# Mixer output projection in seven products: chains spread over steps, and the order of the first product

## The chip, the cores and the metric

The kernel runs on one core of one Trainium2 chip, as one launch. The metric is the device time of that launch in microseconds (us), the median of several runs. The profile names the core's engines PE (matrix products; PEld is its weight load), DVE, ACT and POOL (elementwise work), and SP, whose queue issues the kernel's DMAs.

## What is computed

One layer of a hybrid encoder: a sparse attention and a state-space (SSD) mixer read the same input, their outputs are projected, merged under sigmoid gates and projected once more, and a gated feed-forward block follows, all over 1024 positions of width 1024 in float32. The part around the change is this (the reference, cut):

```python
y_a = sparse_mla_attention(...) @ w_o_attn
y_b = ssd_mixer(...) @ w_o_ssd          # ssd_mixer ends in rmsnorm over 2048 columns
mix = (sigmoid(g_a) * y_a + sigmoid(g_b) * y_b) @ w_out
x = x + gate_m * rmsnorm(mix, post_norm_mix)
h2 = rmsnorm(x, pre_norm_ffn) * (1.0 + scale_f) + shift_f
u_gate, u_up = split(h2 @ w_ffn_in, 2)
f = (silu(u_gate) * u_up) @ w_ffn_out
x = x + gate_f * rmsnorm(f, post_norm_ffn)
```

## The kernel before

Activations lie transposed: 128 channels on the partitions, 512 positions (one half) in a tile. A float32 operand of a product is split in two parts, a high part rounded to the matrix engine's format (ACT writes it) and the rest (DVE or POOL subtracts); a product of four 128-row blocks is then twelve matmuls of 128x512: high by high, high by low, low by high (`P3`).

**The stage.** After the SSD mixer, `y @ w_o_ssd` is made by a seven-product scheme, with block products named 1, 5, 6, 7, 3, 4, 2, and `merged @ w_out` in two passes A and B, one per half of the positions. A list `seq` holds 88 steps `(name, m, h)`: `m` is the block of output channels, `h` the half of the four-plus-four row blocks that the step multiplies. Each step is twelve matmuls. The order is 1, 5, 6, 7, 3 (steps 0 to 39, eight each), A (40 to 55), 4 and 2 (56 to 71), B (72 to 87). Before the change product 1 runs its steps as (m=0,h=0), (m=0,h=1), (m=1,h=0) and so on.

**One pass of the loop** (`for i in range(len(seq))`, L1374 on) issues, in this order: the load of a SSD output tile for the next product (`y_act`, into pool EV), the raw weights of step i+5 (`wo_load`; four raw buffers), whatever `pre[i]` holds (loads of gates, of the attention branch, of x), the twelve matmuls of step i (`wo_mm`), the weight sum of step i+3 (`wo_sum`, DVE), the high part of the loaded tile (ACT, L1386), the split of the weights of step i+2 (`wo_split`: ACT `whi`, POOL `wlo`; three buffers each), then whatever `post[i]` holds, and last the low part of the loaded tile (DVE, L1391).

**Order.** The whole loop, and before the change also the preload in front of it (raw weights of steps 0 to 4, the eight tile pairs of product 1, the weight splits of steps 0 and 1), stands under `in_order` for PE, ACT, DVE, POOL and SP: each engine gets these instructions in exactly the order in which the code issues them. Outside of `in_order` a planner orders instructions by their place in the code and by when it reckons that they are ready; it may weave the fixed chain with the end of the SSD mixer, which is not under `in_order`.

**What `post` holds before.** Each of these is issued whole in one pass:

- `merge`: DVE multiplies by the gate (L1282), POOL or DVE adds the attention branch (L1283), ACT makes the high part `mgh`, DVE the low part `mgl` (through `split`, L243 and L244). Sixteen of them, eight before A and eight before B.
- `gate_fn`: ACT sigmoid, POOL multiplies by `rys` (L1274). `rys_make` at steps 4 and 6: the SSD norm's sums on PE (`rstd`, L257), a DVE and a POOL instruction for the reciprocal root, four PE transposes that spread it (`rspread`, L268), ACT copies it (L1307). The sums come from `ysq`, which the SSD mixer's last chunks still add to (L1071).
- `mixed`: ACT copies an output of A or B and squares it (L1299, L1300), DVE adds the squares (L1302).
- `x_first` (q0+2 to q0+12, where q0 = 56 is the first step of product 4): DVE scales (L1314), DVE or POOL adds x (L1315), ACT squares (L1316), DVE sums (L1318), SP stores. It needs `prm`, made by `rstd` at q0 and `rspread` at q0+1.
- `h_first` (b0+1 to b0+8, b0 = 72): DVE scales by `pr2` (L1323; its `rstd` and `rspread` at q0+14 and q0+15), ACT high part (L1160), DVE low part (L1161), ACT shift in place (L1163): the input of the FFN.

The gates and x wait in pool Q (26 tiles), which also holds the sixteen split tiles of products 5, 7 and 4. PSUM has three banks in one pool (`bank_d`) and five in another (`bank`); product 1's output tiles take three of the first and one of the second.

Of the kernel before, what the change touches and what calls it, by code (L numbers as in the profile page):

```python
# [65 lines left out]
def build(tc, a, dbg=None, stop=99, slots=None):  # L66
# [1090 lines left out]
    def ffn_input(b, t, h2):  # L1157
        if b == 0:
            hi, lo = H_("h2h", dt=F32R), H_("h2l", dt=F32R)
            S.activation(hi, h2, AF.Identity, bias=mod[:, 24 + t:25 + t])  # L1160
            V.scalar_tensor_tensor(lo, h2, mod[:, 24 + t:25 + t], f(hi), op0=OP.add, op1=OP.subtract)  # L1161
            X[("11", "21")[t // 4]][t % 4] = hi, lo
        S.activation(h2, h2, AF.Identity, bias=mod[:, 24 + t:25 + t])  # L1163

# [115 lines left out]
    def merge(x, t, y, eng):  # L1280
        g = gates.pop((x, t))
        V.tensor_tensor(g, y, g, op=OP.mult)  # L1282
        eng.tensor_tensor(g, g, yas.pop((x, t)), op=OP.add)  # L1283
# [29 lines left out]
    def x_first(t):  # L1313
        V.scalar_tensor_tensor(mixA[t], mixA[t], gm[:, t:t + 1], keep["prm"], op0=OP.mult, op1=OP.mult)  # L1314
        (V if t % 2 else G).tensor_tensor(x1[t], mixA[t], x1[t], op=OP.add)  # L1315
        S.activation(mixA[t], x1[t], AF.Square)  # L1316
        if t:
            V.tensor_tensor(mixA[t], mixA[t], sq_["x"], op=OP.add)  # L1318
# [9 lines left out]

    end = {n: [pos[n, m, 1] + 1 for m in range(4)] for n in PRODUCT}
    for m in range(4):  # L1330
        post[end["1"][m]].append(lambda m=m: S.activation(c11[m], U(m), AF.Copy))
        post[end["5"][m]].append(lambda m=m: S.activation(c22[m], outs["5", m], AF.Copy))
        post[end["6"][m]].append(lambda m=m: V.tensor_tensor(c12[m], U(m), c22[m], op=OP.add))
        post[end["7"][m]].append(lambda m=m: V.tensor_tensor(c22[m], U(m), c22[m], op=OP.add))
        post[end["3"][m]].append(lambda m=m: V.tensor_tensor(c12[m], outs["3", m], c12[m], op=OP.add))
        post[end["2"][m]].append(lambda m=m: V.tensor_tensor(c11[m], outs["2", m], c11[m], op=OP.add))
# [6 lines left out]
    a0, b0 = pos["A", 0, 0], pos["B", 0, 0]
    for q, m in enumerate((0, 1, 2, 3)):
        plan_merge("B", 4 + m, end["4"][m], a0 - 1 + 2 * q, a0 + 1 + 2 * q, lambda m=m: U(m), G)
        plan_merge("B", m, end["2"][m], a0 + 7 + 2 * q, a0 + 9 + 2 * q, lambda m=m: c11[m], V)
    for t in range(8):
        for n, i0 in (("A", a0), ("B", b0)):
            post[min(i0 + 2 * t + 2, len(seq) - 1)].append(lambda n=n, t=t: mixed(n, t))
    q0 = pos["4", 0, 0]  # L1350
    post[q0].append(lambda: kept_as("rm", lambda: rstd([sq_["A"]], D)))
    post[q0 + 1].append(lambda: kept_as("prm", lambda: rspread(keep["rm"])))
    for t, at in enumerate((2, 3, 5, 6, 8, 9, 11, 12)):
        pre[q0 + at - 4].append(lambda t=t: x_ask(t))
        post[q0 + at].append(lambda t=t: x_first(t))
    post[q0 + 14].append(lambda: kept_as("r2", lambda: rstd([sq_["x"]], D)))
    post[q0 + 15].append(lambda: kept_as("pr2", lambda: rspread(keep["r2"])))
# [4 lines left out]
    X = {n: [None] * 4 for n in ("11", "21", "22", "1", "2", "3", "4")}  # L1362
    with in_order(mybir.EngineType.PE, mybir.EngineType.Activation, mybir.EngineType.DVE,
                  mybir.EngineType.Pool, mybir.EngineType.SP):
        for i in range(4):
            wo_load(i)
        for j in range(8):
            y_act("1", j)
            if j < 2:
# [4 lines left out]
        for i in range(len(seq)):  # L1374
            if i + 1 in feeds:
                y_act(*feeds[i + 1])
            wo_load(i + 5)
            for fn in pre[i]:
                fn()
            wo_mm(i)  # L1380
            wo_sum(i + 3)
            if i in feeds:
                n, j = feeds[i]
                hi, lo = ((H_, Q)[PRODUCT[n] % 2]("a" + k, None, F32R) for k in "hl")
                r = als.pop((n, j))
                S.activation(hi, r, AF.Copy)  # L1386
            wo_split(i + 2)
            for fn in post[i]:
                fn()
            if i in feeds:  # L1390
                V.tensor_tensor(lo, r, f(hi), op=OP.subtract)  # L1391
# [122 lines left out]
    with in_order(mybir.EngineType.PE):  # L1514
# [7 lines left out]
        for t in range(8):  # L1522
            ffn_input(1, t, y1[t])
# [279 lines left out]
```

## Time and profile before

| | |
|---|---|
| median of 3 runs | 2474.64 us (2472.56 to 2478.26) |
| the profiled execution | 2472.58 us |
| its span, first to last instruction | 2470.8 us |
| TensorE clock granted, mean of the span | 0.983 |
| busy: PE, DVE, ACT, POOL | 95%, 66%, 51%, 44% |

The span is cut by the profile from the first to the last instruction of the program; 1.8 us of the execution's time lie around it. Busy shares count matmuls from issue to end, and two in a row overlap, so a stage is better judged by the number of matmuls in it. The views used below are the page, the table by stretches of time, the timeline, and the instruction groups of a stretch ("xN" is a count; behind the bar stand the busy time, the mean of one in ns, and the idle time of the engine just before these instructions, with what ended it).

### The profile page before, as it was taken

What the parts mean: (1) busy time and instruction counts of PE and PEld (TensorE: products, weight loads), DVE (VectorE), ACT (ScalarE), POOL (GpSimd) and SP (SyncE); (2) the same over time, 40 slices, a digit from 0 to 9 for tenths busy, and PEclk for the clock granted to TensorE, in tenths of its full rate; (3) what the DMA queues carried; (4) which work ended last, traced back from release to release, by engine and by line L of the source; (5) the groups of instructions that cost most, each with busy time, mean ns of one, the idle gap of its engine ahead of it and who ended that gap; (6) DMA issues with size and microseconds to landing.
All of it is one profiled execution on the core that took longest, in us unless ns stands there. A gap on an engine that the chain in (4) does not pass through costs nothing. (4 is left out here: it accounts for less than half of the span.)

```text
span 2470.8 us, 35232 instructions
## 1 busy us (share of the span) xinstructions
PE 2355.7 (95%) x11782; PEld 1898.6 (77%) x11782; DVE 1640.7 (66%) x3150; ACT 1267.5 (51%) x2440; POOL 1099.1 (44%) x869
## 2 busy tenths in 40 slices
PE   7999999999999999999999986989899999999997
PEld 5888888887888877777777765767678788888877
DVE  4467775697765566765667775864557777556786
ACT  3456665667355554555666664534456222335442
POOL 1421112222344346732445433766368555554465
PEclk9999999999999999999999998999999999999999
DMA  7123112422323223314779776646365555328665
GB/s 267 65 89 126 63 66 94 154 90 95 105 95 105 88 101 103 104 49 133 224 246 310 251 233 216 230 154 200 98 234 174 184 176 182 124 99 290 229 213 167
DMA packets 238918, 384.54 MB, mean 156 GB/s; under 512 B 23649, under 2 KB 91921, under 8 KB 238737
## 3 DMA queue, kind: packets, MB, share of 16 engines
q1 hardware_dynamic: 238016, 381.72, 46.5%
q8 instruction: 93, 1.52, 0.3%
q14 instruction: 89, 0.72, 0.1%
q10 hardware_dynamic: 720, 0.58, 0.1%
HBM read 284.13 MB, written 101.21 MB: 156 GB/s over the span
## 5 line engine op out<-in xcount | busy, mean ns | idle before, releaser
L150 POOL TENSOR_TENSOR wlo<-wraw,whi 128x512 fp32r<-128x512 f32 x146 | 200.1, 1371 | 501.6 <-ACT whi L149 459.5
L1412 PE MATMUL p<-xh,wr 128*128 128x512 f32 x880 | 274.1, 389 | 1.9 <-DVE u L1479 1.9
L1406 POOL TENSOR_TENSOR wr<-a,wr 128x512 fp32r<-128x512 f32 x110 | 156.3, 1429 | 125.1 <-ACT wr L1405 94.5
L244 POOL TENSOR_TENSOR wlo<-wraw,whi 128x512 fp32r<-128x512 f32 x97 | 139.1, 1439 | 127.1 <-ACT whi L243 111.4
L1412 PEld LDWEIGHTS p<-xh,wr 128*128 128x128 f32 x880 | 165.2, 188 | 36.7 <-DVE u L1479 2.4
L1412 PE MATMUL p<-xl,wr 128*128 128x512 f32 x440 | 171.2, 389 | 0.0
L149 ACT ACTIVATE whi<-wraw 128x512 fp32r<-128x512 f32 x146 | 91.3, 627 | 122.3 <-issue 39.5
L777 ACT ACTIVATE lg<-lg,mx 128x256 f32<-128x256 f32 (+7 forms) x128 | 98.6, 771 | 100.3 <-DVE mx L774 96.8
L1405 ACT ACTIVATE wr<-a 128x512 fp32r<-128x512 f32 x110 | 68.5, 629 | 144.5 <-PE p L1412 122.9
L1258 PE MATMUL pos<-ah,whi 128*128 128x512 f32 x224 | 94.1, 420 | 21.9 <-ACT whi L243 14.9
L1412 PE MATMUL p<-h2h,wr 128*128 128x512 f32 x352 | 113.3, 398 | 0.0
L244 POOL TENSOR_TENSOR wlo<-ws,whi 128x512 fp32r<-128x512 f32 x57 | 84.7, 1490 | 61.3 <-ACT whi L243 55.8
L637 ACT ACTIVATE junk<-acc,cand__2182 128x1024 bf16<-128x1024 f32 (+2 forms) x96 | 86.2, 898 | 45.7 <-DVE cand__2182 L680 29.9
L1583 PE MATMUL pfo<-ah,wlo 128*128 128x512 f32 x264 | 103.2, 391 | 1.9 <-POOL wlo L244 1.9
L588 DVE SCALAR_TENSOR_TENSOR acc<-rel,widx,acc 128x384 f32<-128x384 f32 (+2 forms) x90 | 87.0, 986 | 24.7 <-ACT rel L583 24.5
L1583 PE MATMUL pfo<-ah,whi 128*128 128x512 f32 x264 | 103.0, 390 | 0.4 <-ACT whi L243 0.4
L1583 PE MATMUL pfo<-al,whi 128*128 128x512 f32 x264 | 102.7, 389 | 0.0
L583 ACT ACTIVATE rel<-prel 128x512 f32<-128x512 f32 (+3 forms) x160 | 77.2, 524 | 48.1 <-PE prel L582 44.5
L315 POOL TENSOR_TENSOR adaw<-adaw,cs 128x512 f32<-128x512 f32 x64 | 66.5, 1042 | 78.0 <-DMA adaw<-ada_w 70.7
L1258 PE MATMUL pos<-ah,wlo 128*128 128x512 f32 x224 | 94.1, 420 | 6.9 <-POOL wlo L244 6.5
L1412 PEld LDWEIGHTS p<-xl,wr 128*128 128x128 f32 x440 | 82.6, 188 | 17.0
L1672 DVE TENSOR_TENSOR al<-al,ah 128x512 fp32r<-128x512 f32 x66 | 71.3, 1082 | 34.1 <-ACT ah L1667 31.8
(604 smaller groups left out, 7500.8 us busy)
## 6 DMA issues: line engine op xcount, KB each, us to landing
wraw<-w_in SPq DMA_DIRECT2D x130, 256.0 KB, 2.6
a<-w_ffn_in SPq DMA_DIRECT2D x120, 256.0 KB, 3.2
al<-d_a SPq DMA_DIRECT2D x77, 256.0 KB, 4.0
wraw<-w_ffn_out SPq DMA_DIRECT2D x66, 256.0 KB, 3.9
adaw<-ada_w SPq DMA_DIRECT2D x64, 256.0 KB, 2.7
al<-d_ac SPq DMA_DIRECT2D x32, 512.0 KB, 4.5
wraw<-w_o_ssd SPq DMA_DIRECT2D x56, 256.0 KB, 3.5
al<-d_y SPq DMA_DIRECT2D x56, 256.0 KB, 4.3
```

What stands on the lines that cost most here:

```text
L149: behind(S.activation(hi[:, :kt], raw[:, :kt], AF.Copy))
L150: behind(G.tensor_tensor(lo[:, :kt], raw[:, :kt], f(hi[:, :kt]), op=OP.subtract))
L244: (lo_eng or V).tensor_tensor(lo, src, f(hi), op=OP.subtract)
L583: S.activation(rel[:, 512 * b:512 * b + w_], pr[:, 0:w_], AF.Relu)
L588: V.scalar_tensor_tensor(acc[i][:, 0:n], rel[:, 0:n], ws, acc[i][:, 0:n], op0=OP.mult, op1=OP.add)
L637: S.activation(jk, y, AF.Sign, scale=-1.0, bias=a_, accum_out=o)
L777: S.activation(lg[:, 0:n], lg[:, 0:n], AF.Exp, scale=-1.0, bias=m, accum_out=mx[:, 3:4])
L1258: T.matmul(p, w[wi][:, q], xs[k][xi], start=n in "1532AB" and h == 0 and q == 0 and x == 0, stop=h == 1 and q == 3 and x == 2, skip_group_ ...
L1406: G.tensor_tensor(w[:, 1], src, f(w[:, 0]), op=OP.subtract)
L1412: T.matmul(p, w[:, wi, i], X[x][i][xi], start=start and i == 0 and k == 0, stop=i == 3 and k == 2, skip_group_check=True)
L1583: T.matmul(o, w[wi][:, P * m:P * m + P], x[xi][:, cl], start=j == 0 and k == 0, stop=j == NP - 1 and k == 2)
L1672: V.tensor_tensor(lo, r, f(hi), op=OP.subtract)
```

## The change

Four things change, all in this stage.

1. Product 1 runs its steps as all four `m` with h=0, then all four with h=1. So steps 0 to 3 read only the first four tile pairs of the SSD output.
2. The preload stands ahead of `in_order`. The loop runs four passes longer, for parts that come after the last step.
3. Every chain of `post` is cut in parts which are issued in successive passes. A merge: multiply at i, add at i+1, high and low part at i+2 (nearer together for the last ones before A and B). The gate's scaling by `rys` comes one pass after the sigmoid. `mixed`: the sum one pass after the squares. `x_first`: five parts in five passes, starting one or two passes later. `h_first`: scale, then high and low part, then shift, in three passes, from q0+20 on (before: b0+1 = q0+17).
4. Each normaliser is split: `rstd` at i, `rspread` at i+2; `rys` is copied at i+3. They stand at steps 5 and 9 (before: 4 and 6), at q0+1 (q0) and q0+17 (q0+14).

```diff
     FIRST, LAST = 1, 0
-    seq = [(n, m, h) for part, ms in (("15673", 4), ("A", 8), ("42", 4), ("B", 8)) for n in part for m in range(ms) for h in BS]
+    seq = [("1", m, h) for h in BS for m in range(4)]
+    seq += [(n, m, h) for part, ms in (("5673", 4), ("A", 8), ("42", 4), ("B", 8)) for n in part for m in range(ms) for h in BS]
...
+    def at(i, fn, *args):
+        post[i].append(lambda: fn(*args))
...
-    def merge(x, t, y, eng):
-        g = gates.pop((x, t))
-        V.tensor_tensor(g, y, g, op=OP.mult)
-        eng.tensor_tensor(g, g, yas.pop((x, t)), op=OP.add)
-        MG.setdefault(x, {})[t] = split(H_, g, "mg")
+    def merge(x, t, y):
+        V.tensor_tensor(gates[x, t], y(), gates[x, t], op=OP.mult)
+
+    def merge_add(x, t, eng):
+        eng.tensor_tensor(gates[x, t], gates[x, t], yas.pop((x, t)), op=OP.add)
+
+    def merge_hi(x, t):
+        hi, lo = H_("mgh", dt=F32R), H_("mgl", dt=F32R)
+        S.activation(hi, gates[x, t], AF.Copy)
+        MG.setdefault(x, {})[t] = hi, lo
+
+    def merge_lo(x, t):
+        hi, lo = MG[x][t]
+        V.tensor_tensor(lo, gates.pop((x, t)), f(hi), op=OP.subtract)
...
+        at(fn, gate_fn, x, t)
+        at(fn + 1, gate_scale, x, t)
+        pre[i - 5].append(lambda: ya_load(x, t))
+        at(i, merge, x, t, y)
+        at(i + steps[0], merge_add, x, t, eng)
+        at(i + steps[1], merge_hi, x, t)
+        at(i + steps[1], merge_lo, x, t)
...
+    def normaliser(i, name, sq, n):
+        at(i, kept_as, ("r", name), lambda: rstd([sq()], n))
+        at(i + 2, kept_as, name, lambda: rspread(keep["r", name]))
...
-    post[4].append(lambda: rys_make(FIRST))
-    post[6].append(lambda: rys_make(LAST))
+    for i, b in ((5, FIRST), (9, LAST)):
+        normaliser(i, ("pry", b), lambda b=b: ysq[b], D_INNER)
+        at(i + 3, rys_keep, b)
...
+        plan_merge("A", 4 + m, end["7"][m] + 1, G_LOAD[m], G_FN[m], lambda m=m: c22[m], G, (1, 2))
+        plan_merge("A", m, end["3"][m], G_LOAD[4 + m], G_FN[4 + m], lambda m=m: c12[m], V if m > 1 else G,
+                   ((1, 2), (1, 2), (0, 1), (0, 0))[m])
+        plan_merge("B", 4 + m, end["4"][m], a0 - 1 + 2 * m, a0 + 1 + 2 * m, lambda m=m: U(m), G, (1, 2))
+        plan_merge("B", m, end["2"][m], a0 + 7 + 2 * m, a0 + 9 + 2 * m, lambda m=m: c11[m], V,
+                   ((0, 1), (0, 1), (0, 1), (0, 0))[m])
     for t in range(8):
...
+            at(i0 + 2 * t + 2, mixed, n, t)
+            at(i0 + 2 * t + 3, mixed_sum, n, t)
+    normaliser(q0 + 1, "prm", lambda: sq_["A"], D)
+    for t, i in enumerate((4, 5, 7, 8, 9, 11, 12, 13)):
+        pre[q0 + i - 4].append(lambda t=t: x_ask(t))
+        for n, fn in enumerate((x_scale, x_add, x_square, x_sum, x_store)):
+            at(q0 + i + n, fn, t)
+    normaliser(q0 + 17, "pr2", lambda: sq_["x"], D)
     for t in range(8):
-        post[b0 + 1 + t].append(lambda t=t: h_first(t))
+        at(q0 + 20 + t, h_scale, t)
+        at(q0 + 21 + t, ffn_hi, t)
+        at(q0 + 21 + t, ffn_lo, t)
+        at(q0 + 22 + t, ffn_shift, t)
...
+    for i in range(4):
+        wo_load(i)
+    for j in range(8):
+        y_act("1", j)
+        acts["1"][j] = split(H_, als.pop(("1", j)), "a")
+        if j < 2:
+            wo_split(j)
+    y_act(*feeds[0])
+    wo_load(4)
     with in_order(mybir.EngineType.PE, mybir.EngineType.Activation, mybir.EngineType.DVE,
                   mybir.EngineType.Pool, mybir.EngineType.SP):
...
-        for i in range(len(seq)):
+        for i in range(len(post)):
...
-            wo_mm(i)
+            if i < len(seq):
+                wo_mm(i)
```

More of the change, by code (lines that the diff above doesn't have):

```diff
@@ L1155, in residual_steps, with ffn_hi, ffn_lo, ffn_shift @@
         yield
[L1157 to L1162, printed above, removed]
+    X = {n: [None] * 4 for n in ("11", "21", "22", "1", "2", "3", "4")}
+    def ffn_hi(t):
+        hi, lo = H_("h2h", dt=F32R), H_("h2l", dt=F32R)
+        S.activation(hi, x1[t], AF.Identity, bias=mod[:, 24 + t:25 + t])
+        X[("11", "21")[t // 4]][t % 4] = hi, lo
+    def ffn_lo(t):
+        hi, lo = X[("11", "21")[t // 4]][t % 4]
+        V.scalar_tensor_tensor(lo, x1[t], mod[:, 24 + t:25 + t], f(hi), op0=OP.add, op1=OP.subtract)
+    def ffn_shift(t, x=None):
+        h2 = (x or x1)[t]
         S.activation(h2, h2, AF.Identity, bias=mod[:, 24 + t:25 + t])
@@ L1271, in gate_fn, with gate_scale @@
     def gate_fn(x, t):
-        g = gates[x, t]
-        S.activation(g, g, AF.Sigmoid)
-        G.tensor_tensor(g, g, rys[FIRST if x == "A" else LAST], op=OP.mult)
+        S.activation(gates[x, t], gates[x, t], AF.Sigmoid)
+    def gate_scale(x, t):
+        G.tensor_tensor(gates[x, t], gates[x, t], rys[FIRST if x == "A" else LAST], op=OP.mult)
     def ya_load(x, t):
@@ L1303, in mixed, with rys_keep @@
         sq_[n] = sq
-    def rys_make(b):
+    def rys_keep(b):
         rys[b] = wp.tile([P, 4, P], F32, name="rys", tag=("uraw", "uh")[b], bufs=1).rearrange("p k m -> p (k m)")
-        S.activation(rys[b], rbank(ysq[b], D_INNER), AF.Copy)
+        S.activation(rys[b], keep["pry", b], AF.Copy)
     def x_ask(t):
@@ L1343, in build @@
[L1343 to L1346, printed above, removed]
+        at(end["1"][m], lambda m: S.activation(c11[m], U(m), AF.Copy), m)
+        at(end["5"][m], lambda m: S.activation(c22[m], outs["5", m], AF.Copy), m)
+        at(end["6"][m], lambda m: V.tensor_tensor(c12[m], U(m), c22[m], op=OP.add), m)
@@ new lines, in build @@
+        at(end["7"][m], lambda m: V.tensor_tensor(c22[m], U(m), c22[m], op=OP.add), m)
+        at(end["3"][m], lambda m: V.tensor_tensor(c12[m], outs["3", m], c12[m], op=OP.add), m)
+        at(end["2"][m], lambda m: V.tensor_tensor(c11[m], outs["2", m], c11[m], op=OP.add), m)
+    for i, b in ((5, FIRST), (9, LAST)):
+        normaliser(i, ("pry", b), lambda b=b: ysq[b], D_INNER)
+        at(i + 3, rys_keep, b)
+    G_LOAD, G_FN = (4, 5, 6, 7, 15, 16, 17, 18), (10, 11, 13, 14, 18, 19, 21, 22)
@@ new lines, in build @@
+    a0, b0, q0 = pos["A", 0, 0], pos["B", 0, 0], pos["4", 0, 0]
+    for m in range(4):
+        plan_merge("A", 4 + m, end["7"][m] + 1, G_LOAD[m], G_FN[m], lambda m=m: c22[m], G, (1, 2))
[4 more added lines that the diff above has]
+                   ((0, 1), (0, 1), (0, 1), (0, 0))[m])
@@ L1347, in build @@
     for t in range(8):
         for n, i0 in (("A", a0), ("B", b0)):
[L1349 to L1355, printed above, removed]
@@ L1522, in build @@
         for t in range(8):
[L1523 removed]
+            ffn_shift(t, y1)
         ffn_sums(x1, y1)
```

45 lines of the change are left out of this document (13 added, 32 removed).

## The prediction

> **What bounds the kernel now.** The page first: PE is the busiest engine by far. I then cut the stage of the change with the table by stretches of time, counting only its matmuls (L1258; a count may take in one that overlaps an edge).
>
> ```profile
> PE 2355.7 (95%) x11782; PEld 1898.6 (77%) x11782; DVE 1640.7 (66%) x3150; ACT 1267.5 (51%) x2440; POOL 1099.1 (44%) x869
> ```
>
> ```profile
> core 0: us, PE busy (x) PEld busy (x), PEclk, DMA share, GB/s
> 1450.20:1514.90 64.70, 7.16 (x24) 4.25 (x23) 0.87 0.53 170
> 1514.90:1549.20 34.30, 27.67 (x96) 21.32 (x97) 0.84 0.84 285
> 1549.20:1595.50 46.30, 46.30 (x206) 38.24 (x205) 1.00 0.65 212
> 1595.50:1652.20 56.70, 48.00 (x181) 34.84 (x180) 0.94 0.46 155
> 1690.30:1706.00 15.70, 14.23 (x62) 11.17 (x62) 1.00 0.39 123
> 1706.00:1758.50 52.50, 40.55 (x145) 28.97 (x144) 0.90 0.48 160
> 1772.10:1808.40 36.30, 29.81 (x121) 21.71 (x119) 1.00 0.30 99
> ```
>
> In the third stretch nothing stalls: 17 steps of twelve matmuls take 46.3 us, so a step costs 46.3/17 = 2.72 us, a matmul 0.227. By that price the others are too long. Steps 2 to 9: 34.3 where 8 x 2.72 = 21.8, excess 12.5. Steps 27 to 41: 56.7 against 40.8, excess 15.9. Steps 56 to 60: 15.7 against 13.6, excess 2.1. Steps 61 to 72: 52.5 against 32.6, excess 19.9. Steps 78 to 87: 36.3 against 27.2, excess 9.1. Together 59.5 us; what lies between ran at 2.72. Before that, from 1450.2 to 1514.9, only steps 0 and 1 ran. What follows the stage runs PE without a gap, so a stage that ends earlier ends the kernel earlier:
>
> ```profile
> 1860.00:1900.00 40.00, 40.00 (x178) 33.14 (x177) 33.62 (x29) 22.84 (x43) 36.00 (x24) 1.00 0.47 159
> ```
>
> **The start (order of product 1, preload, rys).** The timeline of the stage's beginning:
>
> ```profile
> 1448.61 2.19 ACT L243 ACTIVATE ah<-al 128x512 fp32r<-128x512 f32 x4
> ...
> 1463.70 0.51 PE L1258 MATMUL pos<-ah,whi 128*128 128x512 f32 x1 [4.40 <-ACT ah L243]
> ...
> 1483.79 0.66 PE L1025 MATMUL pyd<-al,X 128*64 128x256 f32 x4 [4.11 <-DVE al L986]
> 1493.86 0.66 PE L1025 MATMUL pyd<-al,X 128*64 128x256 f32 x4 [3.38 <-DVE al L986]
> 1502.91 0.50 PE L1258 MATMUL pos<-ah,whi 128*128 128x512 f32 x1 [2.57 <-ACT ah L243]
> ...
> 1506.56 0.40 PE L1258 MATMUL pos<-ah,wlo 128*128 128x512 f32 x1
> ...
> 1512.41 0.63 ACT L1049 ACTIVATE ysqt<-zy 128x512 f32<-128x512 f32 x1 [4.43 <-POOL zy L1046]
> ...
> 1513.82 0.42 DVE L1071 TENSOR_TENSOR ysq<-ysq,ysqt 128x256 f32<-128x256 f32 x1
> ...
> 1514.27 0.61 ACT L243 ACTIVATE whi<-wraw 128x512 fp32r<-128x512 f32 x1
> ...
> 1514.93 0.80 PE L1258 MATMUL pos<-ah,whi 128*128 128x512 f32 x1 [7.98 <-ACT whi L243]
> ...
> 1523.42 0.63 ACT L1386 ACTIVATE ah<-al 128x512 fp32r<-128x512 f32 x1 [5.98 <-DMA al<-d_y]
> ...
> 1525.43 0.95 PE L257 MATMUL p<-ones,ysq 128*128 128x1 f32 x8
> ...
> 1528.73 0.65 PE L268 MATMUL prn<-ident,r 128*128 128x128 f32 x4 [2.35 <-POOL r L262]
> ...
> 1529.59 0.63 PE L1258 MATMUL pos<-al,whi 128*128 128x512 f32 x1
> 1530.01 0.63 PE L1258 MATMUL pos<-ah,wlo 128*128 128x512 f32 x1
> ...
> 1532.57 0.45 PE L1258 MATMUL pos<-ah,wlo 128*128 128x512 f32 x1
> ```
>
> PE finishes step 1 at 1506.6, when the last SSD tile of product 1 is there, then stands 8 us for the weights of step 2: ACT has their split in its fixed order behind the SSD mixer's last squares (1512.41), which wait for POOL. Later it stands 2.35 us in the middle of `rys`, and comes back slow: two matmuls start 0.42 us apart, not 0.227, until about 1532.6.
>
> After: steps 0 to 3 need only tiles 0 to 3, split by about 1451 (1448.61 and on), so their 48 matmuls and the weight splits behind them go into the idle gaps of the SSD chunks. Step 4 waits for the eighth tile as step 1 did and ends at 1506.6, step 5 at 1509.3. Then comes a new wait: `rstd` of `rys` now stands behind step 5 on PE, and needs `ysq`, last added to at 1513.82 + 0.42 = 1514.2; steps 6 on queue behind it. It ends at 1515.2. Steps 6 to 9 cost 10.9, one set of transposes 0.65, the second `rstd` 0.95, and a slow restart like that of 1529 to 1532.6, some 8 matmuls x 0.2 = 1.6 us: step 10 begins at 1529.3. The eighth tile of product 5, converted by 1523.42 + 0.63, is needed only at the end of step 9 and does not bind. To this I add 2 us because 24 more matmuls (5.4 us) and five weight splits share the SSD mixer's last chunks, whose period is 10.1 us (1483.79 to 1493.86) with 3.4 to 4.1 us of PE idle in each: the bounds are 0 and the 5.4 us. So 1531.3 against 1549.2, **18 us** gained; bounds 21.5 (no delay, no slow restart) and 0 (the planner leaves the order as it is).
>
> **The merges into A (steps 27 to 41).** Instruction groups of that stretch, ACT, DVE and POOL:
>
> ```profile
> L243 ACT ACTIVATE mgh<-sgb 128x512 fp32r<-128x512 f32 x8 | 5.1, 631 | 29.0 <-POOL sgb L1283 26.3 <-DVE sgb L1283 2.7
> ```
>
> ```profile
> L244 DVE TENSOR_TENSOR mgl<-sgb,mgh 128x512 fp32r<-128x512 f32 x8 | 5.5, 692 | 17.6 <-ACT mgh L243 17.6
> L1335 DVE TENSOR_TENSOR acc<-pos,acc 128x512 f32<-128x512 f32 x4 | 2.7, 682 | 0.0
> ```
>
> ```profile
> L1283 POOL TENSOR_TENSOR sgb<-sgb,yal 128x512 f32<-128x512 f32 x7 | 9.0, 1288 | 4.3 <-DVE sgb L1282 4.3
> ```
>
> Eight merges cost ACT 29.0 us of standing and DVE 17.6, and the next `whi` and weight sums wait behind them. With a pass between the parts these waits go. What is late next is the throughput of DVE and POOL together. Where both are full the timeline shows:
>
> ```profile
> 1557.56 1.78 DVE L1190 TENSOR_TENSOR ws<-ws,wraw 128x512 f32<-128x512 f32 x1
> 1559.27 1.78 DVE L1391 TENSOR_TENSOR al<-al,ah 128x512 fp32r<-128x512 f32 x1
> ```
>
> ```profile
> 1557.05 3.44 POOL L244 TENSOR_TENSOR wlo<-ws,whi 128x512 fp32r<-128x512 f32 x2
> ```
>
> A DVE instruction on two SBUF tiles takes 0.69 us when POOL is still and 1.78 beside it; in alternation a pair goes every 1.70 us. Counting the changed code, passes 27 to 41 issue 21 POOL instructions (15 `wlo`, 6 adds), 35 such DVE ones (7 low parts of tiles, 10 weight sums, 8 multiplies, 8 low parts of merges, 2 adds) and 8 that read PSUM. So 21 pairs x 1.70 = 35.7, plus 14 x 0.69 = 9.7, makes 45.4 us if the PSUM readers lie beside POOL, 50.8 if none does (8 x 0.68, as L1335). PE wants 40.8, and weights are split two steps ahead, a lead of 5.4 less 1.9 for `whi` and `wlo` (0.61 + 1.29): 3.5. So 1.1 to 6.5 us of stall remain; I take 4, nearer the middle since both engines mix the two. The steps between 10 and 26 keep their contents and their 2.72.
>
> **Residual and merges into B (steps 56 to 72).** The same view of 1706.0 to 1758.5, then the timeline:
>
> ```profile
> L243 ACT ACTIVATE mgh<-sgb 128x512 fp32r<-128x512 f32 x6 | 3.8, 632 | 18.0 <-POOL sgb L1283 9.4 <-DVE sgb L1283 8.6
> L1316 ACT ACTIVATE acc<-xr 128x512 f32<-128x512 f32 x6 | 3.8, 631 | 14.5 <-POOL xr L1315 8.2 <-DVE xr L1315 6.3
> ```
>
> ```profile
> 1702.02 0.33 SPq L1311 DMA_DIRECT2D xr<-xT  x1
> ...
> 1709.75 0.33 SPq L1311 DMA_DIRECT2D xr<-xT  x1
> ...
> 1716.44 0.50 PE L1258 MATMUL pos<-ah,whi 128*128 128x512 f32 x1 [1.62 <-ACT whi L243]
> ...
> 1749.29 1.05 PE L257 MATMUL p<-ones,acc 128*128 128x1 f32 x8 [2.87 <-DVE acc L1318]
> ```
>
> ACT stands 32.5 us for merges and residual. The SP queue also stands, some 7 us between two loads of x, because pool Q is full (8 gates, 16 split tiles, 2 of x), and the weights behind come late. Asked for two passes later, the fourth x meets the first free tiles of product 4 (step 62), so weights are then loaded four steps ahead. The 2.87 us of `rstd` goes, as it stands three passes later. Next is the crowd in passes 64 to 72: 13 POOL instructions, 24 DVE ones on SBUF, 10 that read PSUM: 22.1 + 11 x 0.69 = 29.7, to 36.5 with all ten, against 24.5 + 3.5. Stall 1.7 to 8.5; I take 5. The last merge into B is still one chain in pass 72, five instructions of 0.6 to 0.7 us and perhaps one hold by POOL of 1.1 (1.78 less 0.69), 4.4 us; step 73 reads its high part 2.72 + 9 x 0.227 = 4.8 us in, its low part one matmul later. With the handing over between engines I take 1 us (bounds 0 and 2).
>
> **FFN input (78 to 87) and normalisers.** Three passes apart, its parts need one POOL and at most two DVE instructions on SBUF a pass: 1.70 + 0.34 + 0.74 is about 2.72; stall 0 (bound 4). PE's own part of a normaliser stays, 0.95 + 0.65: from step 10 on one set of transposes and two whole ones, 3.9 us. I leave 1.5 us for slow clock.
>
> **The sum.** From step 10 to the end: 78 x 2.72 = 212.2, + 3.9 + 4 + 5 + 1 + 1.5 = 227.6 us, against 1808.4 - 1549.2 = 259.2 now: 31.6 gained. With the start 49.6. The profiled execution took 2472.58 us (span 2470.8 and 1.8 around it), 2.06 below the median of the runs shown, 2474.64; 2472.6 - 49.6 = 2423.0, and on the median **2425 us**.
>
> **Rivals.**
>
> A. *DVE and POOL bind harder.* If pairs do not alternate so neatly, each costs its full 0.69 + 1.29 = 1.98: the two crowds then take 51.3 and 33.3 us, with half of the PSUM readers uncovered 54.0 and 36.7, which leaves stalls of 9.7 and 8.7, 9 more together than reckoned: 2434. For it: POOL is 9 tenths full at 1860 to 1900 too. Against: the 1.70 us. The Trainium skill, SBUF — State Buffer, section "SBUF: two separate sides", says that a DVE instruction with two SBUF inputs and a GpSimd one exclude each other for the whole instruction, "the other fully blocks"; by that rule the sum is this rival's. The trace agrees in kind (1.78 for 0.69) but not in the full length.
>
> B. *The start does not move*: the planner again puts step 2's or 4's splits behind the SSD mixer's end, or the new `rstd` wait is longer. Then 18 us are missing: 2443. For it: the 7.98 us come from the planner's order alone. Against: the fixed chain on ACT no longer begins with the eight tiles.
>
> C. *Slower: pool Q starves SP.* Gates are freed one or two passes later. If each of the eight loads of x waits as 1702.02 to 1709.75 did (7.7 us, 61.6 together), the gain of 49.6 turns into a loss of 12, 2487 on the median; it decides from the seventh such wait on. Against: sixteen tiles come free in steps 62 and 63, which serve the loads from the fourth on.
>
> **How the numbers follow.** Forecast 0.61, A 0.2, B 0.13, C 0.03; 0.03 for parts cancelling to nothing. If no stall were left (all but the 3.9 us), 11.5 more would go: 2413.5; with the start's 3.5 too, 2410. At the other end B with the PSUM readers uncovered (2443 + 6) makes 2449. The range is 2410 to 2449. About 0.2%, 5 us, is what a measurement can tell from no change: faster 0.94, same 0.03, slower 0.03.
>
> **What would show it.** Right: four steps of L1258 before 1475; step 10 near 1531; ACT's idle time before `mgh` and before the squares of x near nothing; DVE instructions of 1.78 us in rows between steps 28 and 36; 2.72 us steps from 78 on; the stage's last matmul near 1759. Wrong: PE waiting for `whi` behind an SSD instruction on ACT; chunk periods well over 10 us; SP gaps of 7 us at the loads of x; PE waiting for DVE at `rstd` of step 5 for longer than 5 us.

## The result, and the profile after

The changed kernel takes 2441.75 us (median of 4 runs, 2435.38 to 2444.39) against 2473.6 us before in the same session: a ratio of 0.9864, interval 0.9841 to 0.9888. Its profiled execution took 2441.79 us, 30.8 less than the one before. The forecast was 2425.0 with 2410 to 2449 around it: the sign and the range held, but 49.6 us were forecast and 30.8 came.

First the page of the changed kernel, its busy times:

```profile
PE 2343.9 (96%) x11782; PEld 1894.8 (78%) x11782; DVE 1659.6 (68%) x3151; ACT 1267.6 (52%) x2440; POOL 1102.7 (45%) x868
```

Then the table by stretches, cut at the steps, for the stage's matmuls alone (now L1269). The rows are steps 0 and 1, 2 to 9, 10 to 26, 27 to 41, 42 and 43, 61 to 71, 72 to 77, 78 to 87; the columns are the stretch, its length, PE, PEld, the granted clock and DMA.

```profile
core 0: us, PE busy (x) PEld busy (x), PEclk, DMA share, GB/s
1451.60:1508.60 57.00, 5.98 (x24) 4.33 (x24) 0.88 0.56 178
1508.60:1538.05 29.45, 26.39 (x96) 19.53 (x97) 0.89 0.82 269
1538.05:1585.95 47.90, 47.21 (x204) 38.15 (x205) 1.00 0.78 260
1585.95:1637.50 51.55, 45.54 (x181) 33.15 (x181) 0.97 0.53 178
1637.50:1644.80 7.30, 7.30 (x25) 5.85 (x24) 0.73 0.57 180
1692.50:1722.45 29.95, 29.95 (x133) 24.59 (x131) 1.00 0.68 228
1722.45:1750.10 27.65, 20.13 (x73) 14.68 (x73) 0.88 0.30 95
1750.10:1778.70 28.60, 27.56 (x121) 22.34 (x119) 1.00 0.43 140
```

Steps 61 to 71 took 49.7 us before and run at 2.72 each now; steps 78 to 87 took 36.2. The stage ends at 1778.7 instead of 1808.3, and what follows takes 661.3 us of the span (662.4 before): nothing is lost behind the stage. The shortfall lies inside, term by term. The forecast's figures are those of its working: 2.72 a step, 0.65, 1.6 and 1.6 for the normalisers in the second, fifth and sixth row, stalls of 4 us at A and 6 in the row of B.

| part | forecast, us | measured, us |
|---|---|---|
| stage's begin to step 10 | 81.1 | 86.5 (99.0 before) |
| steps 10 to 26 | 46.9 | 47.9 |
| steps 27 to 41 (merges into A) | 44.8 | 51.5 |
| steps 42, 43 | 5.4 | 7.3 |
| steps 44 to 60 | 47.8 | 47.7 |
| steps 61 to 77 (residual, merges into B) | 53.8 | 57.6 |
| steps 78 to 87 | 27.2 | 28.6 |
| slow clock, anywhere | 1.5 | in the rows above |

The measured column adds up to 327, the forecast to 308.5. Steps 86 and 87 are 3.40 each because three FFN matmuls stand in each; before, only in one of them.

**The start.** The changed kernel's timeline where step 2 begins:

```profile
1503.79 0.63 ACT L1049 ACTIVATE ysqt<-zy 128x512 f32<-128x512 f32 x1 [4.85 <-POOL zy L1046]
...
1506.09 0.63 ACT L1049 ACTIVATE ysqt<-zy 128x512 f32<-128x512 f32 x1 [0.87 <-POOL zy L1046]
...
1507.42 0.61 ACT L1429 ACTIVATE ah<-al 128x512 fp32r<-128x512 f32 x1
...
1507.94 0.61 ACT L243 ACTIVATE whi<-wraw 128x512 fp32r<-128x512 f32 x1
...
1508.61 0.79 PE L1269 MATMUL pos<-ah,whi 128*128 128x512 f32 x1 [6.54 <-ACT whi L243]
```

Read upwards: PE waits for the weights of step 2; ACT splits them only after the high part of the first tile of product 5, which heads its fixed order; and that stands behind the SSD mixer's last squares, which wait for POOL. Steps 2 and 3 did not run early.

Step 2 nevertheless starts 6.3 us earlier in the span than before (1508.61 against 1514.93), because the SSD mixer's last squares come 6.3 us earlier (1506.09 against 1512.41). In the kernel before, the fixed order of PE holds two waits for tiles of product 1 among the SSD chunks (4.40 and 2.57 us, at 1463.70 and 1502.91); the changed kernel has none there. The order of the start alone brings that (e2: 1507.6; e1, without it: 1514.1). That these two waits were what held the SSD mixer back is argued, not tested.

**The ends of the two crowds.** PE's timeline in step 33, in steps 41 and 42 and in steps 72 and 73, then DVE's before the end of step 73:

```profile
1608.53 0.50 PE L1269 MATMUL pos<-al,whi 128*128 128x512 f32 x1 [1.32 <-DVE al L1434]
...
1635.76 0.80 PE L1269 MATMUL pot<-mgh,whi 128*128 128x512 f32 x1 [2.91 <-ACT mgh L1300]
1636.48 0.80 PE L1269 MATMUL pot<-mgl,whi 128*128 128x512 f32 x1
1637.08 0.63 PE L1269 MATMUL pot<-mgh,wlo 128*128 128x512 f32 x1
1637.51 0.63 PE L1269 MATMUL pot<-mgh,whi 128*128 128x512 f32 x1
1637.93 0.63 PE L1269 MATMUL pot<-mgl,whi 128*128 128x512 f32 x1
...
1724.91 0.50 PE L1269 MATMUL pot<-mgh,wlo 128*128 128x512 f32 x1 [1.71 <-POOL wlo L244]
...
1732.89 0.50 PE L1269 MATMUL pot<-mgh,whi 128*128 128x512 f32 x1 [3.18 <-ACT mgh L1300]
...
1735.31 1.87 PE L257 MATMUL p<-ones,acc 128*128 128x1 f32 x8 [0.48 <-DVE acc L1352]
```

```profile
1715.54 1.77 DVE L1352 TENSOR_TENSOR acc<-acc,acc 128x512 f32<-128x512 f32 x1
...
1729.43 0.68 DVE L1375 TENSOR_TENSOR acc<-pos,acc 128x512 f32<-128x512 f32 x1
1730.15 1.29 DVE L1293 TENSOR_TENSOR sgb<-acc,sgb 128x512 f32<-128x512 f32 x1
1731.48 0.69 DVE L1296 TENSOR_TENSOR sgb<-sgb,yal 128x512 f32<-128x512 f32 x1
1732.87 0.69 DVE L1305 TENSOR_TENSOR mgl<-sgb,mgh 128x512 fp32r<-128x512 f32 x1 [0.70 <-ACT mgh L1300]
1733.47 1.77 DVE L1352 TENSOR_TENSOR acc<-acc,acc 128x512 f32<-128x512 f32 x1
```

Product 2's last output is complete when step 71 ends, at 1722.5. DVE adds it (L1375) at 1729.43, seven us or two and a half passes late, and has no idle time in front of it. The last merge follows, and PE waits 3.18 us for it; before that, in step 72, it waits 1.71 us for a low part of weights from POOL. At A the last merge holds PE in the same way in step 41 (2.91 us), and in step 33 it is the low part of the last tile of product 3 (1.32 us). Behind the wait of step 41 PE is slow: matmuls 0.43 us apart, so that step 42, which waits for nothing, takes 4.61 us.

The waits that the change was to remove shrank. The instruction groups of steps 27 to 41, to be held against the 29.0 and 17.6 us of before:

```profile
L1305 DVE TENSOR_TENSOR mgl<-sgb,mgh 128x512 fp32r<-128x512 f32 x8 | 8.3, 1040 | 4.8 <-ACT mgh L1300 4.7
...
L1300 ACT ACTIVATE mgh<-sgb 128x512 fp32r<-128x512 f32 x8 | 5.0, 628 | 11.8 <-POOL sgb L1296 6.0 <-DVE sgb L1296 5.8
```

### The profile page after: what moved, and what is told of

Same layout as the page of the kernel before. It is cut to its first block, busy times and chain, and to the rows that moved or that the text cites. A ratio compares the mean times of both kernels' runs of the same rounds, so it can differ in the third digit from the quotient of the medians.

```text
span 2440.0 us, 35233 instructions
## 1 busy us (share of the span) xinstructions
PE 2343.9 (96%) x11782; PEld 1894.8 (78%) x11782; DVE 1659.6 (68%) x3151; ACT 1267.6 (52%) x2440; POOL 1102.7 (45%) x868
## 5 line engine op out<-in xcount | busy, mean ns | idle before, releaser
L244 POOL TENSOR_TENSOR wlo<-ws,whi 128x512 fp32r<-128x512 f32 x57 | 84.6, 1487 | 56.4 <-ACT whi L243 51.4
L637 ACT ACTIVATE junk<-acc,cand__2182 128x1024 bf16<-128x1024 f32 (+2 forms) x96 | 86.2, 898 | 45.8 <-DVE cand__2182 L680 29.9
L1269 PE MATMUL pos<-ah,whi 128*128 128x512 f32 x224 | 89.5, 400 | 7.3 <-ACT whi L243 7.3
L1269 PE MATMUL pos<-ah,wlo 128*128 128x512 f32 x224 | 90.0, 402 | 2.8 <-POOL wlo L244 2.5
```

The costliest lines, as they stand in the source:

```text
L244: (lo_eng or V).tensor_tensor(lo, src, f(hi), op=OP.subtract)
L637: S.activation(jk, y, AF.Sign, scale=-1.0, bias=a_, accum_out=o)
L1269: T.matmul(p, w[wi][:, q], xs[k][xi], start=n in "1532AB" and h == 0 and q == 0 and x == 0, stop=h == 1 and q == 3 and x == 2, skip_group_ ...
```

## The experiments

Every kernel was timed beside the kernel before, and ratios are to that (the changed kernel: 0.9864). Intervals are about 0.2% wide to each side, so single fixes can't be ranked by time; they are read from the lengths of their stretches, in us (to about 0.1), from the starts of the steps' first matmuls in each trace. "Behind" is what the span has after the stage's last matmul.

| kernel | ratio (interval) | 0-9 | 27-41 | 42-43 | 72-77 | behind |
|---|---|---|---|---|---|---|
| before | | 99.0 | 56.8 | 5.5 | 16.4 | 662.4 |
| changed | 0.9864 (0.9841 to 0.9888) | 86.5 | 51.5 | 7.3 | 27.7 | 661.3 |
| e1 chains only | 0.9891 (0.9865 to 0.9918) | 93.9 | 51.7 | 7.6 | 27.7 | 661.8 |
| e2 start only | 0.9968 (0.9958 to 0.9979) | 95.5 | 56.9 | 5.4 | 16.4 | 661.1 |
| e3 feeds late | 0.9842 (0.9822 to 0.9862) | 81.6 | 50.7 | 7.1 | 27.6 | 662.4 |
| e4 adds on DVE | 0.9850 (0.9830 to 0.9869) | 87.9 | 49.6 | 6.8 | 27.3 | 662.2 |
| e5 late use | 0.9853 (0.9834 to 0.9872) | 87.9 | 47.0 | 7.8 | 28.3 | 664.3 |
| e6 all fixes | 0.9822 (0.9803 to 0.9840) | 80.2 | 44.1 | 8.3 | 28.4 | 663.5 |
| e7 no sum of x | 0.9844 (0.9826 to 0.9863) | 89.4 | 51.4 | 7.6 | 23.2 | 664.9 |
| e8 no differences for 3 | 0.9831 (0.9814 to 0.9847) | 88.5 | 45.0 | 7.1 | 27.6 | 660.1 |
| e9 e6, normaliser + 4 | 0.9815 (0.9798 to 0.9833) | 80.9 | 43.4 | 8.2 | 21.0 | 667.9 |
| e10 e9, x stretched | 0.9819 (0.9798 to 0.9840) | 80.3 | 44.0 | 8.2 | 20.5 | 668.3 |
| e11 x stretched alone | 0.9891 (0.9866 to 0.9917) | 88.0 | 51.4 | 7.4 | 24.2 | 668.9 |
| e12 e6, normaliser + 2 | 0.9796 (0.9782 to 0.9810) | 81.4 | 44.2 | 8.2 | 21.5 | 662.3 |

Steps 61 to 71 take 29.9 or 30.0 us in every kernel with the spread chains (48.5 in e2).

### e1 and e2: the chains, the start

e1 keeps the chains and takes the two parts of the start back (the edit of e1, cut); e2 is the kernel before with those two parts.

```diff
-    seq = [("1", m, h) for h in BS for m in range(4)]
-    seq += [(n, m, h) for part, ms in (("5673", 4), ...
+    seq = [(n, m, h) for part, ms in (("15673", 4), ...
...
+    with in_order(...):
         for i in range(4):
             wo_load(i)
         for j in range(8):
             y_act("1", j)
...
-    with in_order(...):
         for i in range(len(post)):
```

> The changed kernel with product 1 in its old order (row pairs 0-3 and 4-7 in turn for each m) and the preload back under the fixed order; chains and normalisers stay spread. If start and chains add up (the changed trace: step 10 is 11.2 us earlier, the stage's end 30.3), this keeps 30.3 - 11.2 = 19.1 us of the gain: step 10 near 1549, median near 2454.5. If the chains were worth the forecast 31.6 us and the new start costs them something later, it gives near 2442, no slower than the full change. If the chains gain only together with the early start, it is near 2470.

> The kernel before with the new order of product 1 and the preload ahead of the fixed order; chains and normalisers as before, so the sums of rys stand at steps 4 and 6. If the parts add up: 2473.6 - 11.2 = 2462.4. If the normaliser at step 4 now waits for the last ysq (about 1514) with steps 5 and on behind it, some 3 us less gain: 2465. If a start that comes earlier is eaten by the crowded passes later: 2473.

e1's ratio is a gain of 1.09%, e2's of 0.32%; together 1.41%, where the full change has 1.36%: the parts add up. e1's own time, 2450.27 us, beside 2478.25 before, was lower than the 2454.5 expected, because its start, too, is 5.1 us shorter than before: the later normalisers of `rys` alone bring that (0.65 of it only because the second spread now stands behind step 10). e2 shows why. PE's timeline there:

```profile
1520.77 0.95 PE L257 MATMUL p<-ones,ysq 128*128 128x1 f32 x8
1527.93 0.69 PE L268 MATMUL prn<-ident,r 128*128 128x128 f32 x2 [6.22 <-POOL r L262]
```

With sums and spread as near together as before, PE stands 6.22 us at the spread of `rys`. It was 2.35 before. That is the second case of e2's expectation, which gave 2465; on the 2473.6 that it started from, e2's ratio makes 2465.7. So of the 12.5 us at the start, 5.1 belong to the normalisers (e1), 3.5 to the order (e2), and 3.9 appear when both are there; the last figure is uncertain, since kernels with the same start differ by up to 2.9 us (86.5 to 89.4 in the table).

### e3: what heads ACT's fixed order

```diff
...
+    for i in range(8):
+        feeds[i] = [("5", 2 * i - 8), ("5", 2 * i - 7)] if i > 3 else []
...
```

> The changed kernel with one difference: the eight tiles of product 5 are loaded and split two per pass in passes 4 to 7 instead of one per pass in passes 0 to 7, so that ACT's fixed order begins with the weight splits of steps 2 to 5 and not with a tile that needs a place in pool Q. Theory (the head of ACT's fixed order held steps 2 and 3 behind the SSD mixer): steps 0 to 3 all run before 1500, step 4 starts near 1507 when the eighth tile is there, step 10 near 1528 to 1532 instead of 1538.1, and the time falls by 6 to 10 us against the changed kernel, to about 2434. Rival 1 (PE has no room in the SSD chunks: 24 more matmuls delay the chunks by as much): step 10 between 1534 and 1538, 2440. Rival 2 (splits of tiles, two per pass, hold the weights of steps 6 to 9): step 4 near 1507 but step 10 not before 1536.

ACT's timeline, then PE's:

```profile
1463.88 0.62 ACT L243 ACTIVATE whi<-wraw 128x512 fp32r<-128x512 f32 x1
...
1465.43 0.63 ACT L243 ACTIVATE whi<-wraw 128x512 fp32r<-128x512 f32 x1
...
1470.20 0.61 ACT L243 ACTIVATE whi<-wraw 128x512 fp32r<-128x512 f32 x1
```

```profile
1467.95 0.39 PE L1269 MATMUL pos<-ah,wlo 128*128 128x512 f32 x1
...
1512.15 1.83 PE L1037 MATMUL pyo<-ld,state 128*128 128x256 f32 x4
1513.63 0.59 PE L1269 MATMUL pos<-ah,whi 128*128 128x512 f32 x1
```

The tile was what held the splits: those of steps 3 and 4 now come at 1463.88 and 1465.43, step 2 runs at once, and the 6.54 us wait is gone. But step 3, with its weights there, stands on PE behind the SSD mixer's last product (L1037): the planner's order on PE. So the expectation failed at step 3. In the five kernels with this edit (e3, e6, e9, e10, e12) the stretch to step 10 takes 80.2 to 81.6 us, in the six others with the changed start 86.5 to 89.4. The edit is worth about 7 us there, though in e3 the stage began 3.5 us later than in the changed kernel, and step 10 only 1.3 earlier. There is a price, too, as its first rival had it: with this edit the SSD mixer's last product starts 57.0 us after the stage's begin (1512.15) instead of 49.3 in the changed kernel (1500.93). The twelve matmuls of step 2, 2.7 us, do not alone account for these 7.7 us. Why the SSD mixer is later, and why the planner puts the tile and step 3 there (a place in pool Q was a guess), stays open.

### e4: which price a DVE instruction has beside POOL

```diff
-        plan_merge("A", 4 + m, ..., lambda m=m: c22[m], G, (1, 2))
-        plan_merge("A", m, ..., lambda m=m: c12[m], V if m > 1 else G,
+        plan_merge("A", 4 + m, ..., lambda m=m: c22[m], V, (1, 2))
+        plan_merge("A", m, ..., lambda m=m: c12[m], V,
```

> The changed kernel with the six adds of the merges into A that POOL does given to DVE. If a DVE instruction beside POOL costs what the pair rate says (1.70 us a pair, 0.69 alone): 15 x 1.70 + 26 x 0.69 = 43.4 instead of 45.4 us for the two-input work of passes 27 to 41, steps 27 to 41 take about 49.5 us instead of 51.5, and the time is 2 us lower. If DVE's own number of instructions is what binds (six more of at least 0.69 us in its order): steps 27 to 41 take about 55.5 and the time is 4 us higher. Within 1 us: neither, the handing over between ACT, DVE and POOL sets the pace.

The table by stretches for all engines, steps 27 to 41 of the changed kernel, then of e4 (PE, PEld, DVE, ACT, POOL):

```profile
1585.95:1637.50 51.55, 45.54 (x181) 33.15 (x181) 45.62 (x46) 19.43 (x34) 32.71 (x22) 0.97 0.53 178
```

```profile
1586.45:1636.00 49.55, 44.45 (x181) 34.61 (x180) 46.37 (x52) 19.49 (x34) 22.91 (x16) 0.96 0.56 186
```

Six more instructions cost DVE 0.75 us in all, since it waits less for POOL, which sheds 9.8; the stretch is 2 us shorter, as the pair price of 1.70 us said. DVE's number of instructions alone does not bind. By the Trainium skill (SBUF — State Buffer, section "SBUF: two separate sides": each excludes the other for the whole instruction) a pair would cost 0.69 + 1.29 = 1.98 and the six adds would bring 6 x (1.98 - 2 x 0.69) = 3.6 us, an estimate from the durations of this case; the trace shows 2. The five kernels of the table that leave these passes as the changed one has them (changed, e1, e3, e7, e11) take 50.7 to 51.7 us for the stretch, so the difference is clear of their spread, if not by much.

### e5, e7: what comes late at step 73

e5 runs the first three output blocks of A and of B with h=0 first, so that the last merges are read two steps later:

```diff
-    seq += [(n, m, h) for part, ms in (("5673", 4), ("A", 8), ("42", 4), ("B", 8)) for n in part for m in range(ms) for h in BS]
+    for part, ms, k in (("567", 4, 1), ("3", 4, 1), ("A", 8, 3), ("42", 4, 1), ("B", 8, 3)):
+        for n in part:
+            seq += [(n, m, h) for h in BS for m in range(k)] + [(n, m, h) for m in range(k, ms) for h in BS]
...
-            at(i0 + 2 * t + 2, mixed, n, t)
-            at(i0 + 2 * t + 3, mixed_sum, n, t)
+            at(i0 + max(t + 4, 2 * t + 2), mixed, n, t)
+            at(i0 + max(t + 5, 2 * t + 3), mixed_sum, n, t)
```

> The changed kernel with another order of the first steps of A and of B: the first three output blocks run their first half (h=0) one after the other and only then their second halves, so that the merges t=0..3, which come last, are read two steps (5.4 us) later. Theory (the last merges are late because DVE is two to three passes behind at the end of a crowd, and PE then also restarts slowly): the waits at the first h=1 step of A (3.3 us and a slow step behind) and of B (7 us, rstd aside, and a slow step behind) shrink by up to 5.4 us each, 8 to 10 us in all: about 2432. Rival 1 (the whole DVE, POOL and ACT queues are behind, the weight splits too): the waits move to the weights of the steps that are now in front, gain under 3 us: 2439 to 2442. Rival 2 (what is late is one chain of fixed length from the last step of product 2): gain 5.4 at each place, the same as the theory, but with DVE not behind by a pass before it.

e7 replaces the add in `x_sum` by nothing, so its normaliser of x leaves out seven of eight squares:

> The changed kernel without the seven DVE adds that sum the squares of x (the normaliser of x then takes the last square alone; seven DVE instructions on SBUF tiles fewer in passes 64 to 74). Theory (DVE and POOL together are over capacity in passes 64 to 72): 7 x 0.69 to 7 x 1.78 us of DVE go, the wait at step 73 (9.7 + 4.5 us for steps 73 and 74) falls by 5 to 8 us: about 2435. Rival (the last merge into B is a chain of its own length behind step 71, whatever else DVE does): steps 72 to 74 stay within 1.5 us of 19.0, 2441.

At A steps 27 to 43 fall from 58.8 to 54.8 us: there the last merge was the wait. What is left there is shorter waits for weights (0.36 us in step 42, 0.41 and 0.70 in step 43), as the first rival had it in part. At B nothing is gained (28.3), so 4 us came of the 8 to 10 expected. PE's timeline of e5 shows why:

```profile
1719.90 0.50 PE L1271 MATMUL pot<-mgh,wlo 128*128 128x512 f32 x1 [1.71 <-POOL wlo L244]
...
1730.30 1.87 PE L257 MATMUL p<-ones,acc 128*128 128x1 f32 x8 [5.10 <-DVE acc L1354]
```

The merge's wait has gone, and `rstd` of x, which follows in PE's order, waits 5.10 us for the last sum of x from the same late DVE. In the changed kernel this second wait hid behind the first, at 0.48 us. e7 makes DVE earlier, and both shrink; its PE timeline at the same place:

```profile
1729.55 0.50 PE L1269 MATMUL pot<-mgh,whi 128*128 128x512 f32 x1 [1.51 <-ACT mgh L1300]
1730.27 0.50 PE L1269 MATMUL pot<-mgl,whi 128*128 128x512 f32 x1 [0.22 <-DVE mgl L1305]
1730.84 1.34 PE L257 MATMUL p<-ones,acc 128*128 128x1 f32 x8
```

Steps 72 to 77 fall by 4.5 us, a little under the 5 to 8 expected. DVE's add of the last output now comes 2.5 us after the end of step 71 instead of 7.0: the backlog of DVE, not a chain of fixed length, is the larger part of it.

### e8: the crowd before A

e8 leaves out the weight differences of product 3:

```diff
-            V.tensor_tensor(w, raw, w, op=OP.subtract)
+            w = raw
```

> The changed kernel without the eight weight differences of product 3 on DVE (it then multiplies by the raw weights; eight DVE instructions on SBUF tiles fewer in passes 29 to 36). Theory (DVE and POOL over capacity from pass 27 on, the delay adding up until step 42): 8 x 0.69 = 5.5 us of DVE at the least go, steps 27 to 42 take 50 us or less instead of 56.1, with the wait at step 33 under 1 us: about 2435. Rival (the waits at steps 33 and 41 are those of single chains: the last tile of product 3, the last merge): steps 27 to 42 within 2 us of 56.1, 2440.

```profile
1586.60:1631.55 44.95, 42.15 (x181) 33.40 (x180) 34.60 (x37) 18.49 (x33) 31.75 (x22) 1.00 0.60 199
```

In this row of all engines for steps 27 to 41, DVE has 11.0 us less (nine instructions: the window cuts its order at another place) and the stretch 6.6. Steps 27 to 42 take 49.3 us, where the theory had 50 or less: over capacity, as it has it. Step 33 fell to 3.78 us from 5.60, and its wait, for the tile alone, to 0.73. Of the 2.91 us at the last merge of step 41, 1.77 were left. DVE's add of product 3's last output comes 2.9 us after the end of step 39 (5.0 in the changed kernel), and from there to the matmul 3.8 us pass in both: the backlog shrank, and the chain behind it did not.

### e6, e9 to e12: the fixes together

e6 has the edits of e3, e4 and e5, and product 3 with two blocks of h=0 first.

> The changed kernel with: the tiles of product 5 two per pass in passes 4 to 7; the six adds of the merges into A on DVE; A and B with three first halves ahead; product 3 with two first halves ahead. If the effects add up: 1.3 us at the start, 2 at the adds, 8 to 10 at A and B, 3 in step 33: 14 to 16 us below the changed kernel, about 2426. If the crowd only passes its delay on (each fix moves the wait to the next step): no lower than 2436.

It measured 2430.83 us beside 2474.15, between the 2426 of effects that add up and the 2436 of a delay that is only passed on. Steps 27 to 41 fall to 44.1, with no wait at step 33; at B it is where e5 was. The next four move the normaliser of x:

```diff
-    normaliser(q0 + 17, "pr2", lambda: sq_["x"], D)
+    normaliser(q0 + 21, "pr2", lambda: sq_["x"], D)
...
-        at(q0 + 20 + t, h_scale, t)
+        at(q0 + 24 + t, h_scale, t)
```

and `ffn_hi`, `ffn_lo`, `ffn_shift` with it. e10 and e11 also have x at q0 + (4, 6, 8, 10, 12, 14, 16, 17); e11 is that on the changed kernel, without the four fixes.

> The kernel with all four fixes (late first use in A, B and 3; adds on DVE; tiles of product 5 two per pass) and the normaliser of x (rstd, spread, FFN input chain) four passes later, the x chain itself where it was. Theory (two things came late at step 73 for one reason: the last merge, and behind it on PE the rstd that waits for the last sum of x; with the merge out of the way rstd stands there alone): steps 72 to 77 lose the rest of their wait, from 27.4 us (19.55 for 72 to 74) to about 20, and the time falls by 5 to 7 us to about 2425. Rival (DVE and POOL are behind until they have done all of it, so the weight splits of steps 74 to 77 wait instead): under 2 us.

> As the run before, with the x chain itself stretched: a tile every second pass (passes 60 to 73 instead of 60 to 69), so that four of its DVE instructions leave passes 64 to 72. Theory (DVE with POOL over capacity there): 4 x 0.69 to 4 x 1.7 us less by pass 72, the weight splits come in time, steps 72 to 77 take 17.5 us or less, 2 to 4 us below the run before: about 2422. Rival (the stretch only moves the same instructions on to passes 73 to 77): the same time as the run before, within 1 us.

> The changed kernel with only the x chain stretched to a tile every second pass, and the normaliser of x and the FFN input chain four passes later; orders of A and B and the adds as changed. Theory (the last merges into B are late only because DVE is behind): with four DVE instructions and rstd out of the way the wait at step 73 falls, steps 72 to 77 from 27.7 us to 20 to 22, about 2435. Rival (the merge chain of its own length): step 73 still waits some 3 us for the high part of a merge and restarts slowly, steps 72 to 77 about 24 to 25, 2438.

Inside the stage the theory of e9 holds: 28.4 to 21.0 us in steps 72 to 77. But its time, 2430.10, is e6's. The gain is handed back behind the stage (667.9 instead of 663.5), where the FFN's first products wait for an input that comes four passes later:

```profile
1765.02 0.50 PE L1459 MATMUL p<-h2l,wr 128*128 128x512 f32 x1 [1.86 <-DVE h2l L1166]
...
1767.38 0.79 PE L1459 MATMUL p<-h2h,wr 128*128 128x512 f32 x1 [1.63 <-ACT h2h L1161]
1768.67 0.80 PE L1459 MATMUL p<-h2l,wr 128*128 128x512 f32 x1 [0.49 <-DVE h2l L1166]
```

Stretching x as well (e10) takes only 0.5 us more from steps 72 to 77, and its time, 2431.70, is e9's within the intervals, as its rival had it. In e11 the stage is 2.3 us shorter than in the changed kernel and 7.6 are lost behind it: its ratio, 0.9891, lies above the changed kernel's 0.9864, though the intervals overlap. Its steps 72 to 77 take 24.2 us, where the theory had 20 to 22 and the rival, a merge chain of its own length, 24 to 25. DVE and PE in step 73 of e11:

```profile
1725.77 0.68 DVE L1375 TENSOR_TENSOR acc<-pos,acc 128x512 f32<-128x512 f32 x1
...
1728.62 0.80 PE L1269 MATMUL pot<-mgh,whi 128*128 128x512 f32 x1 [3.82 <-ACT mgh L1300]
```

The number is the rival's, the mechanism is not. Step 71 ends at 1719.87, and DVE, again without idle time in front, adds its output 5.9 us later; from the add to the matmul 2.9 us pass. In the changed kernel these are 7.0 and 3.5, in e7 2.5 and 3.9. The matmul has its place 4.8 us after step 71, so the chain alone would not hold it. The stretch took only 1.1 us off the backlog.

e12 moves the normaliser by two passes:

> The kernel with all four fixes and the normaliser of x with the FFN input chain two passes later, instead of four (where the last FFN input tiles came 5.5 us too late for the FFN). Theory (rstd stood in front of matmuls that had their operands, and 2 passes are enough to let the sum of x arrive; the FFN input is then late by no more than a pass): steps 72 to 77 near 21 us, the wait behind the stage under 2 us, about 2426. Rival (the sum of x arrives only in step 75 or later, and what the stage gains is lost again at rstd or at the first FFN products): 2430, like the two runs beside it.

2425.81 us beside 2476.75, ratio 0.9796: lower than the changed kernel beyond the intervals, and below e6 and e9 with intervals that overlap. Its table for steps 72 to 77, and PE at their two ends:

```profile
1710.00:1731.45 21.45, 17.98 (x73) 13.08 (x73) 1.00 0.41 124
```

```profile
1712.44 0.50 PE L1271 MATMUL pot<-mgh,wlo 128*128 128x512 f32 x1 [1.70 <-POOL wlo L244]
...
1724.71 0.95 PE L257 MATMUL p<-ones,acc 128*128 128x1 f32 x8
```

`rstd` waits for nothing, the clock stays at 1.00, and behind the stage nothing is lost (662.3). A wait for a low part of weights, 1.70 us, stays.

## Why the prediction was right, and where it was short

- **The sign and the mechanism** held: waits inside chains that were issued whole stood in front of everything later on their engine. Cutting them brings 18.8 us from step 10 on even with the old start (e1's stage from step 10 on against that of before: 240.3 and 259.1). That is a balance: steps 61 to 71 gain 19.8 us, 78 to 87 7.7 and 27 to 41 5.1, while 72 to 77, with the normaliser and the last merges in them, lose 11.3 and 42 and 43 lose 2.1.
- **The start**, 18 us forecast, 12.5 measured (11.2 on the clock of the span, as the stage began 1.4 us later). The step that failed: "their 48 matmuls and the weight splits behind them go into the idle gaps of the SSD chunks". Steps 0 and 1 did, 2 and 3 did not. The forecast's argument against rival B, that the fixed chain on ACT no longer begins with the eight tiles, overlooked what it begins with now: a tile of product 5. It is a mild form of rival B, shown by e3 for ACT; PE's order is a second bar. The sign that the forecast itself named for this, PE waiting for `whi` behind an SSD instruction on ACT, is the 6.54 us wait. The new wait of `rstd` for `ysq` did not show.
- **Merges into A**: 4 us of stall forecast, 10.7 measured (51.5 less 40.8). Of these, 4.6 lie in step 41, 2.9 in step 33 and 3.2 in the others. The size of the work was near: 45.4 us reckoned for DVE with POOL, 45.62 busy measured in the window of these steps, and the pair price stood the test of e4. Wrong was the use of the lead: the sum was set against PE's time plus 3.5 us of lead of the weights. A lead lets PE run on while DVE falls behind, but what stands last in DVE's order, the last merge, has no such lead and meets the backlog, 5.0 us at A. The same holds for the last tile of product 3. The forecast gave that no price at A. Part of it is the merges' own handing over: DVE stood 1.47 and 0.70 us for ACT's high parts just before.
- **Residual and merges into B**: 5 + 1 us forecast in steps 56 to 72, none found up to step 71, 9.8 in steps 72 to 77 (27.7 less 16.3 for six steps and 1.6 for the normaliser): 2.1 in step 72, the rest from step 73 on. The step that failed: "The last merge into B is still one chain in pass 72", priced as if DVE were in that pass then; it was two and a half passes behind (1729.43 against 1722.5), and the sum of x, later still, held `rstd` (e5, e7).
- **The slow clock**: 1.5 us reckoned from step 10 on. Step 42 alone lost 4.61 - 2.72 = 1.9 and step 74 1.7, each without waiting: a stall was priced by its length, without the slow matmuls behind it.
- **FFN input, normalisers, SP** came as forecast: steps of 2.72 from 77 to 85, and no step of 61 to 71 waits for weights that SP brought late, so rival C fell. Rival A's stalls, 9.7 and 8.7 us, are close to the 10.7 and 9.8 that came, but not by its price: in the crowd before A DVE instructions beside POOL still start 1.70 us apart (1616.99, 1618.69, 1620.39), and e4 speaks against the dearer pair. Rival B's time, 2443, is the nearest to the result, but the start is 5.4 us of a shortfall of some 19. That the time lies inside the range is in part luck: its upper end was reckoned from a start that does not move at all and 6 us more of stall, not from the losses that came.

## What to carry to other kernels

Where two engines are over capacity for a while, ask not only whether the total fits beside the bound engine with its lead, but what stands last in their order and who needs it first: the backlog arrives there. Giving that use two more steps took 4 us off at A (e5); a shorter chain was not tried. When a wait is removed, look at what stands next in the same queue and hangs on the same late engine (here a normaliser behind a merge), and at who reads the result when a chain is moved later. An order that is fixed by hand is no earlier than its first instruction.

## What the runs showed of the hardware

- After the 2.91 us wait of the changed kernel PE's matmuls start 0.43 us apart for a while: twelve of them take 5.6 us (1635.76 to 1641.35) instead of 2.7. After e12's 1.70 us wait the clock shows 1.00; after e8's 1.77 us eight matmuls were slow, and after e7's 1.51 us, with `rstd` in between, all twelve of the next step, so the wait's length alone does not decide. The Trainium skill (TensorE: Matmul & The Clock Gate, section "Back-to-back issue gap") has 512 columns divided by 1.2 per ns, 0.427 us, for the slow state, which agrees with 1637.51 to 1637.93. The wait that led to it is shorter than the idle window of about 3.4 us of that page's section "What's actually happening".
- The same instructions can reach the stage at different times. Up to the stage's first matmul e3 and e6 have the same order on PE, ACT and DVE, and it starts at 1455.16 in the one and at 1447.46 in the other. That is more than most single fixes are worth, and why they are read from their stretches.
